# Gated-delta and gMLP decoder layer on one core: sample states loaded by the queue that stores them, right-hand sides of a head pair made together, one query tile earlier in the fill list

## The chip, the core and the metric

The kernel runs on one core of one Trainium2 chip. The metric is the device time of one execution in microseconds; smaller is better. The engines are TensorE (PE, with its weight loads as PEld), VectorE (DVE), ScalarE (ACT), GpSimd (POOL) and SyncE (SP). Each works through its own queue in order. DMA transfers are issued from the queues of SP, POOL and, twice, ACT.

## The reference, cut to what is touched

One layer of a decoder, for a prompt group (one sequence of 512 tokens) and a sample group (8 sequences of 8 new tokens each), which share all weights. The model has 1024 channels, 8 heads of 128 x 128 and float32 throughout.

```
h    = rms_norm(x);  proj = h @ w_in          # q,k,v | z | a,b | u,v | gates
q,k,v = silu(short causal conv of width 4), q and k of unit norm
# gated delta rule, per head, in chunks:
#   S_t = exp(g_t) (I - beta_t k_t k_t^T) S_{t-1} + beta_t k_t v_t^T,   o_t = S_t^T q_t
a_mat = strict_lower(k_beta @ k^T * decay)
sol   = triangular_solve(a_mat + I, [v * beta, k_beta * exp(gc)])
...                                            # scan over chunks; state of every sequence is an output
o_a  = rms_norm(o) * silu(z)
o_b  = u * (tril(W_s) @ layer_norm(v) + b)     # chunked gMLP branch
merged = sigmoid(g_a) * (o_a @ w_proj_a) + sigmoid(g_b) * (o_b @ w_proj_b)
x    = x + rms_norm(merged @ w_out);  x = x + rms_norm(swiglu_ffn(rms_norm(x)))
```

For the sample group the delta rule starts from a stored state, `state_delta`, one 128 x 128 matrix for each of 8 sequences and 8 heads, and returns the updated ones.

## The kernel before

All 576 tokens (64 sample, 512 prompt) stand side by side in the free dimension. Products run in three passes of a high and a low part (`xh`, `xl` against `whi`, `wlo`). A weight tile is 1024 x 128: SP loads it (`wunit_raw`, L261, 512 KB, two buffers `wraw`), ACT makes `whi`, DVE makes `wlo` (`wsplit`, L256 and L124), PE runs 24 matmuls for each of two halves of the tokens (`part`, L282), and the half is evicted from PSUM. PSUM has eight banks: three for weight tiles (`mmps`), five for everything else (`bank`). `ev` (L120) is a ring of seven SBUF tiles for short use: evictions, convolutions, gates, decay rows.

The stretch around the change is the delta branch. `delta(h0)` makes a set of steps for four heads, once for heads 0 to 3 (`dA`), once for 4 to 7 (`dB`). `keys` builds norms and Gram matrices (`decay`, L674, loads a row of decays `gcr` from the DRAM tile `gcd` by POOL, into `ev`). `elim` inverts 32 x 32 blocks on DVE. `combine` stores the result to DRAM, loads it back (`XH` by POOL, `XT` and `XS` by SP) and joins the blocks with small matmuls (L817 first). `scan` runs over the chunks of the prompt. `sample(q)` handles two heads `pr` of the sample group, so there are four calls in all; `both` takes turns between `scan` and `sample`. `output` scales and transposes the result (L975, L984), and `keys2` prepares the second four heads. These are Python generators: `main` steps through them one after the other.

Weight tiles that don't depend on this chain (keys and queries `kq`, values `va` and `vb`, gates `ga` and `gb`, `z`) are put between its steps: `FILL` names for each tile the number of the step of `main` behind which it is traced. Steps 13 to 23 belong to `elim` of `dA`, 24 to 28 to `combine` of `dA`. The order of tracing is a priority. A planner then fixes the order of every queue: on each engine it takes, of what is ready by its own clock and has a free buffer, what was traced first. So a queue's order isn't that of the text, and instructions can run far ahead of their place in it.

`sample(q)` loads four states `Si` (two heads, two halves `z` of four sequences, 256 KB each; four buffers) by `ld`, which is SP's queue. They are read by L880, updated in place and stored to `sd_s` by `st`, which is POOL's queue (L911). A state load of the next call needs a buffer whose store has landed. The update of one head and half is: copies that form W3 (`stack_w`, L720), the right-hand side `we` on DVE (96 x 512, one buffer), one matmul on PE (L907), four updates of 128 x 128 on DVE, the store. The helpers `tt` and `stt` record on L124 and L127, `act` on L136, whoever calls them.

Of the kernel before, what the change touches and what calls it, by code (L numbers as in the profile page):

```python
# [7 lines left out]
F32R = mybir.dt.float32r  # L8
# [4 lines left out]
P = 128  # L13
# [19 lines left out]
def _host_consts():  # L33
# [37 lines left out]
FILL = {  # L71
# [21 lines left out]
def _build(ctx, tc, I, O):  # L93
    nc = tc.nc
    V, S, G, TE = nc.vector, nc.scalar, nc.gpsimd, nc.tensor
    ld = nc.sync.dma_start
    st = nc.gpsimd.dma_start
# [19 lines left out]
    def bank():  # L117
        return pg.tile([P, 512], F32, name="bank", tag="bank")

    def ev(w=T):  # L120
        return evp.tile([P, 611], F32, name="ev", tag="ev")[:, :w]

    def tt(out, a, b, op):
        return V.tensor_tensor(out=out, in0=a, in1=b, op=op)  # L124

    def stt(out, a, s, b, op0, op1):
        V.scalar_tensor_tensor(out=out, in0=a, scalar=s, in1=b, op0=op0, op1=op1)  # L127
# [7 lines left out]
    def act(out, a, f, scale=1.0, accum=None):  # L135
        return S.activation(out=out, in_=a, func=f, scale=scale, accum_out=accum)  # L136
# [25 lines left out]
    def c(n):  # L162
        o, (r, w) = CONST_OFF[n]
        return con[:r, o - co0:o - co0 + w] if n in LATE else con2[:r, o - co1:o - co1 + w]
# [14 lines left out]
    for q in range(2):  # L179
        ps = bank()  # L180
# [54 lines left out]
    for t in range(5):  # L235
# [5 lines left out]
        if t in (1, 2, 3):  # L241
            ps = bank()
# [6 lines left out]
    ps = bank()  # L249
# [96 lines left out]
    pw = ExitStack()  # L346
# [81 lines left out]
    with tc.issue_after(last["v"].ins):  # L428
        ld(out=wsn, in_=I["w_spatial"][0].rearrange("g i j -> i g j"))
        ld(out=bsp.rearrange("p g i -> p (g i)"),  # L430
           in_=I["b_spatial"].rearrange("l g i -> l (g i)")[0].partition_broadcast(P))
# [13 lines left out]
    for q in range(2):  # L445
        ps = bank()
# [4 lines left out]
    ps = bank()  # L451
# [126 lines left out]
    def dt_(shape, nm, bufs=1, dt=F32):  # L578
        return dp.tile(shape, dt, name=nm, tag=nm, bufs=bufs)

    sct = dt_([P, 24, 27], "sct")
    for q in range(3):
        scn = dt_([24, D], "ae", 1)
        st(out=scn, in_=I["state_conv"][0].rearrange("s r f -> (s r) f")[:, q * D:(q + 1) * D])
        ps = bank()
# [20 lines left out]
    def jk():  # L606
        return dt_([P, P], "jk", 1, BF16)
# [42 lines left out]
    def delta(h0):  # L650
# [4 lines left out]
        L = Delta()  # L655
# [60 lines left out]
        def stack_w(w2, z):  # L716
            W3 = dt_([96, 2, P], "W3", dt=F32R)
            rows = slice(32 * z, 32 * z + 32)
            for r in (0, 64) if z == 0 else (0, 32, 64):
                S.copy(out=W3[r:r + 32], in_=w2[rows])  # L720
            tt(W3[32:64], w2[rows], W3[rows], ALU.subtract)
            return W3

# [142 lines left out]
        def sample(q):  # L866
            pr = (2 * q, 2 * q + 1)
            Vps, oS, CC = L.Vps, L.oS, L.CC
            Si = {}
            px = bank()  # L870
            for i, hh in enumerate(pr):
                for z in range(2):
                    Si[i, z] = dt_([P, 4, P], "Si", 4)
                    ld(out=Si[i, z], in_=I["state_delta"][0, 4 * z:4 * z + 4, h0 + hh].rearrange("s k v -> k s v"))
                for o_, f in ((0, F[1, hh]), (8, F[0, hh])):
                    V.tensor_copy(zv[:, o_:o_ + 8, 0:8], f[:, :NS].rearrange("p (s e) -> p s e", e=8))
                for s in range(4):
                    for j in range(4):
                        js = slice(32 * j, 32 * j + 32)
                        TE.matmul(px[js, i * P:(i + 1) * P], lhsT=ZT[:, j * 160 + 32 * s:j * 160 + 32 * s + 32], rhs=Si[i, j % 2][:, s],  # L880
                                  start=(s == 0), stop=(s == 3))
            yield
            rq = dt_([P, 2, P], "rq", 1)
            for i, hh in enumerate(pr):
                stt(rq[:NS, i], px[:NS, i * P:(i + 1) * P], EGN[:NS, 0, h0 + hh:h0 + hh + 1], Vps[:, hh],
                    ALU.mult, ALU.add)
            S.copy(out=rq[NS:P], in_=px[NS:P, 0:256].rearrange("p (a b) -> p a b", b=P))
            for i, hh in enumerate(pr):
                TE.matmul(px[:NS, 256 + i * P:256 + (i + 1) * P], lhsT=XS[:, hh], rhs=rq[:NS, i], start=True, stop=True)
            w2 = rq[:NS]  # L890
            tt(w2, px[:NS, 256:512].rearrange("p (a b) -> p a b", b=P),
               CC[:NS, 0, pr[0]:pr[0] + 2].unsqueeze(2).broadcast_to([NS, 2, P]), ALU.mult)
            for i, hh in enumerate(pr):
                TE.matmul(px[NS:P, i * P:(i + 1) * P], lhsT=L.ans[:, hh], rhs=w2[:, i], start=True, stop=True)
            yield
            tt(oS[:, pr[0]:pr[0] + 2], px[NS:P, 0:256].rearrange("p (a b) -> p a b", b=P), rq[NS:P], ALU.add)
            for hh in pr:
                act(jk()[NS:P], oS[:, hh], AF.Square, accum=SSO[NS:P, 0, h0 + hh:h0 + hh + 1])
            for z in range(2):
                W3 = stack_w(w2, z)  # L900
                for i, hh in enumerate(pr):
                    h = h0 + hh
                    we = dt_([96, 4, P], "we", dt=F32R)
                    tt(we, W3[:, i].unsqueeze(1).broadcast_to([96, 4, P]),
                       c("seqm4").unsqueeze(2).broadcast_to([96, 4, P]), ALU.mult)
                    ps = bank()
                    TE.matmul(ps, lhsT=L.KS[:, z, hh], rhs=we.rearrange("p s v -> p (s v)"), start=True, stop=True)  # L907
                    for s in range(4):
                        sq = 4 * z + s
                        stt(Si[i, z][:, s], Si[i, z][:, s], EGS[:, sq, h:h + 1], ps[:, s * P:(s + 1) * P], ALU.mult, ALU.add)  # L910
                    st(out=O["sd_s"][0, 4 * z:4 * z + 4, h].rearrange("s k v -> k s v"), in_=Si[i, z])  # L911
                yield
# [490 lines left out]
    def tile_mm(t):  # L1403
        T_[t] = Tile_(t, [mmt(), bank()])
        return T_[t].ps
# [11 lines left out]
    ps = tile_mm(0)  # L1417
# [4 lines left out]
    ps = tile_mm(2)  # L1422
# [9 lines left out]
    ps = tile_mm(3)  # L1432
# [7 lines left out]
    ps = tile_mm(4)  # L1440
# [39 lines left out]
    p, q = prs[2].banks("p"), prs[2].banks("q")  # L1480
# [166 lines left out]
```

## Time and profile before

| | |
|---|---|
| median of three runs | 1226.68 us (1223.93 to 1229.81) |
| profiled execution | 1224.94 us, of which the span is 1222.8 us |
| PE busy, share of the span | 1150.5 us, 94% |
| DVE busy | 717.4 us, 59% |
| ACT busy | 569.9 us, 47% |
| POOL busy | 149.7 us, 12% |
| mean granted clock of PE | 0.969 |

The profile is of one execution. The profiled time is the span from the first to the last instruction and 2.1 us around it. In time lines and wait lists a time in brackets is how long the engine stood idle before the instruction, and the name behind `<-` is what ended that. PE's granted clock is given as a share of 2.4 GHz; a stretch at 0.50 runs at 1.2 GHz. The weight-tile stages before 205 us make the normed input, the gMLP branch and its projection; from 205 to 690 us the delta branch runs between weight tiles; then follow `w_proj_a`, `w_out` and from 760 us the feed-forward network.

### The profile page before, as it was taken

How to read it: one execution, taken by the hardware profiler on the slowest of the kernel's cores; microseconds unless marked ns; L12 is line 12 of the kernel's file. 1: busy time of each engine (PE TensorE's matmuls, PEld its weight loads, DVE VectorE, ACT ScalarE, POOL GpSimd, SP SyncE). 2: the span in 40 equal slices, each digit the busy share in tenths (PEclk: the TensorE clock that was granted, in tenths of full speed). 3: DMA queues.
4: the chain of work that ended last, by engine and by line, in shares of the span. 5: the costliest groups of instructions: out<-in, count | busy, mean ns of one | idle time of the engine just before them, and what ended most of it. 6: DMA issues, size and time to landing. Idle time of an engine off the chain costs nothing.

```text
span 1222.8 us, 20426 instructions
## 1 busy us (share of the span) xinstructions
PE 1150.5 (94%) x8144; PEld 1075.6 (88%) x8144; DVE 717.4 (59%) x1386; ACT 569.9 (47%) x1227; POOL 149.7 (12%) x230
## 2 busy tenths in 40 slices
PE   6999999999997999999998998969999999899997
PEld 5999999998996998988997886858999999888885
DVE  4329722557873456767554664667777787661323
ACT  5423323884544773558445443435445445441221
POOL 3001210002000021020010100150111111160001
PEclk9999999999997998998999999988999999999999
DMA  6911344443344354654252744023233333212222
GB/s 163 220 59 37 85 127 112 76 88 110 91 110 94 80 132 91 171 131 89 67 137 72 260 136 138 2 68 87 87 93 92 93 104 103 87 53 86 86 87 78
DMA packets 163011, 124.74 MB, mean 102 GB/s; under 512 B 14096, under 2 KB 145713, under 8 KB 162916
## 3 DMA queue, kind: packets, MB, share of 16 engines
q1 hardware_dynamic: 156226, 103.72, 32.8%
q0 software_dynamic: 6544, 19.64, 4.9%
q8 instruction: 64, 1.05, 0.3%
q14 instruction: 31, 0.25, 0.1%
q10 hardware_dynamic: 146, 0.07, 0.0%
HBM read 106.35 MB, written 17.06 MB: 101 GB/s over the span
## 4 chain that ended last, share of the span: by engine, by line
PE 52%; DMA 7%; DVE 5%; ACT 4%; issue 2%; POOL 0%; POOLq 0%; DVEq 0%; ACTq 0%; SPq 0%
PE mmps L282 13%; PE bank L1305 10%; PE mmps L1305 7%; PE bank L1580 6%; PE mmps L1580 6%; DMA wraw<-w_in 2%; PE bank L1198 2%; PE mmps L1198 1%; DVE wlo L124 1%; DMA wraw<-w_out 1%; ACT whi L256 1%; DMA wraw<-w_proj_a 1%; DMA wraw<-w_ffn_out 1%; PE bank L880 1%; DMA XH<-d 1%
## 5 line engine op out<-in xcount | busy, mean ns | idle before, releaser
L282 PE MATMUL mmps<-xh,whi 128*128 128x256 f32 (+1 forms) x896 | 273.3, 305 | 4.8 <-ACT ev L136 2.9
L282 PE MATMUL mmps<-xh,wlo 128*128 128x256 f32 (+1 forms) x896 | 271.8, 304 | 4.5 <-DVE wlo L124 4.5
L282 PE MATMUL mmps<-xl,whi 128*128 128x256 f32 (+1 forms) x896 | 271.8, 304 | 0.0
L124 DVE TENSOR_TENSOR wlo<-wraw,whi 128x1024 fp32r<-128x1024 f32 x114 | 146.6, 1287 | 208.9 <-ACT whi L256 208.7
L256 ACT CAST whi<-wraw 128x1024 fp32r<-128x1024 f32 x114 | 119.3, 1047 | 209.4 <-PE mmps L282 60.2
L282 PEld LDWEIGHTS mmps<-xh,whi 128*128 128x128 f32 x896 | 174.3, 195 | 7.5 <-ACT ev L136 4.1
L282 PEld LDWEIGHTS mmps<-xh,wlo 128*128 128x128 f32 x896 | 174.4, 195 | 6.3 <-DVE wlo L124 5.6
L282 PEld LDWEIGHTS mmps<-xl,whi 128*128 128x128 f32 x896 | 174.3, 195 | 0.7 <-issue 0.3
L127 DVE SCALAR_TENSOR_TENSOR ev<-ev,fcol 128x600 f32<-128x600 f32 x72 | 60.1, 837 | 1.8 <-ACT ev L136 0.6
L136 ACT ACT_TABLE_LOAD x40 | 51.3, 1283 | 7.6 <-DVE ans L124 3.2
L1305 PE MATMUL bank<-mh,w2hi 128*128 128x288 f32 x156 | 48.0, 308 | 5.3 <-ACT w2hi L256 5.2
L1305 PE MATMUL bank<-mh,w2lo 128*128 128x288 f32 x156 | 47.5, 305 | 2.3 <-DVE w2lo L124 2.3
L136 ACT ACTIVATE ev<-mmps 128x320 f32<-128x320 f32 (+1 forms) x73 | 30.8, 431 | 38.0 <-PE mmps L282 26.4
L1305 PE MATMUL bank<-ml,w2hi 128*128 128x288 f32 x156 | 47.3, 303 | 0.0
L1283 POOL TENSOR_TENSOR wup<-wraw,wup 128x512 f32<-128x512 f32 x20 | 26.2, 1308 | 172.5 <-DVE wup L1283 150.6
L136 ACT ACTIVATE jk<-bank 128x128 bf16<-128x128 f32 (+1 forms) x112 | 31.2, 279 | 17.6 <-PE bank L952 11.6
L282 PE MATMUL mmps<-obl,whi 128*128 128x320 f32 (+1 forms) x128 | 38.6, 303 | 0.0
L282 PE MATMUL mmps<-obh,wlo 128*128 128x320 f32 (+1 forms) x128 | 38.4, 303 | 0.0
L282 PE MATMUL mmps<-oal,whi 128*128 128x320 f32 (+1 forms) x128 | 37.5, 295 | 0.8 <-DVE oal L124 0.8
L282 PE MATMUL mmps<-oah,wlo 128*128 128x320 f32 (+1 forms) x128 | 37.6, 297 | 0.7 <-DVE wlo L124 0.7
L282 PE MATMUL mmps<-oah,whi 128*128 128x320 f32 (+1 forms) x128 | 37.1, 298 | 0.7 <-ACT oah L310 0.7
L282 PE MATMUL mmps<-obh,whi 128*128 128x320 f32 (+1 forms) x128 | 37.6, 303 | 0.0
(501 smaller groups left out, 2996.3 us busy)
## 6 DMA issues: line engine op xcount, KB each, us to landing
wraw<-w_in SPq DMA_DIRECT2D x56, 512.0 KB, 8.2
wup<-w_ffn_in SPq DMA_DIRECT2D x22, 512.0 KB, 4.6
wraw<-w_ffn_out SPq DMA_DIRECT2D x22, 512.0 KB, 3.7
wraw<-w_ffn_in SPq DMA_DIRECT2D x20, 512.0 KB, 4.0
pgd<-ev POOLq DMA_DIRECT2D x16, 288.0 KB, 5.3
ev<-pgd SPq DMA_DIRECT2D x16, 288.0 KB, 7.8
wraw<-w_proj_b SPq DMA_DIRECT2D x8, 512.0 KB, 4.5
Si<-state_delta SPq DMA_DIRECT2D x16, 256.0 KB, 4.9
```

The source lines that it names most:

```text
L124: return V.tensor_tensor(out=out, in0=a, in1=b, op=op)
L127: V.scalar_tensor_tensor(out=out, in0=a, scalar=s, in1=b, op0=op0, op1=op1)
L136: return S.activation(out=out, in_=a, func=f, scale=scale, accum_out=accum)
L256: a = S.copy(out=hi, in_=raw)
L282: TE.matmul(ps, lhsT=a[:, j, :], rhs=b[k][:, HF[hf]], start=(k == 0 and i == 0), stop=(k == nk - 1 and i == 2))
L880: TE.matmul(px[js, i * P:(i + 1) * P], lhsT=ZT[:, j * 160 + 32 * s:j * 160 + 32 * s + 32], rhs=Si[i, j % 2][:, s], start=(s == 0), stop=(s ...
L1198: TE.matmul(ps[q], lhsT=a[k] if t == 0 else a[k][:, o:o + P], rhs=b[k][:, q * 512:(q + 1) * 512], start=(k == 0 and i == 0), stop=(k == KT ...
L1283: (G if g else V).tensor_tensor(out=out, in0=a, in1=b, op=op)
L1305: TE.matmul(ps, lhsT=w[x][:, j], rhs=b[y][:, j], start=(first and j == 0 and i == 0), stop=(j == KH - 1 and i == 2), skip_group_check=not ...
L1580: TE.matmul(ps, lhsT=x[k] if t == 0 else x[k][:, o:o + P], rhs=unit[w][:, a_], start=(k == 0 and i == 0), stop=(k == FT - 1 and i == len(t ...
```

## The change

Three edits. The state loads of `sample` are issued by `st` (POOL's queue) in place of `ld` (SP's). For each half `z` both heads' right-hand sides are made first, the second in an `ev` tile, with a bank of PSUM each; both matmuls follow their right-hand sides, and only then come the updates and stores of both heads. And the sixth entry of `kq` in `FILL`, the query tile of the second head of `dB`, goes from step 28 to step 24.

```diff
     "va": [8, 13, 23, 34],
-    "kq": [16, 20, 20, 24, 24, 28, 32, 33],
+    "kq": [16, 20, 20, 24, 24, 24, 32, 33],
     "ga": [53, 55, 69, 78, 78, 94, 105, 109],
...
                     Si[i, z] = dt_([P, 4, P], "Si", 4)
-                    ld(out=Si[i, z], in_=I["state_delta"][0, 4 * z:4 * z + 4, h0 + hh].rearrange("s k v -> k s v"))
+                    st(out=Si[i, z], in_=I["state_delta"][0, 4 * z:4 * z + 4, h0 + hh].rearrange("s k v -> k s v"))
...
             for z in range(2):
                 W3 = stack_w(w2, z)
+                we = [dt_([96, 4, P], "we", dt=F32R), ev(512).bitcast(F32R)[:96].rearrange("p (s v) -> p s v", v=P)]
+                pw = {}
                 for i, hh in enumerate(pr):
-                    h = h0 + hh
-                    we = dt_([96, 4, P], "we", dt=F32R)
-                    tt(we, W3[:, i].unsqueeze(1).broadcast_to([96, 4, P]),
+                    tt(we[i], W3[:, i].unsqueeze(1).broadcast_to([96, 4, P]),
                        c("seqm4").unsqueeze(2).broadcast_to([96, 4, P]), ALU.mult)
-                    ps = bank()
-                    TE.matmul(ps, lhsT=L.KS[:, z, hh], rhs=we.rearrange("p s v -> p (s v)"), start=True, stop=True)
+                    pw[i] = bank()
+                    TE.matmul(pw[i], lhsT=L.KS[:, z, hh], rhs=we[i].rearrange("p s v -> p (s v)"), start=True, stop=True)
+                for i, hh in enumerate(pr):
+                    h, ps = h0 + hh, pw[i]
                     for s in range(4):
```

## Rows read from the trace of the kernel before

**Rows 1.** A stretch: us; busy us and count by engine, PEclk, DMA share, GB/s.
```profile
205.00:690.00 485.00, 455.32 (x3782) 434.15 (x3781) 301.43 (x744) 281.36 (x744) 47.43 (x76) 0.96 0.43 104
```

**Rows 2.** Waits of PE, 205 to 690 us: total, times, longest.
```profile
PE bank L817 <- DMA XH<-d: 7.2, 1, 7.2
PE bank L907 <- DVE we L124: 5.7, 3, 3.5
...
PE bank L937 <- DVE R L127: 2.8, 1, 2.8
```

**Rows 3.** Time line of PE: start us, us, instruction, idle before it.
```profile
546.62 0.31 PE L282 MATMUL mmps<-xh,wlo 128*128 128x320 f32 x1
548.16 0.51 PE L907 MATMUL bank<-we,KS 96*128 96x512 f32 x1 [1.24 <-DVE we L124]
552.14 0.79 PE L907 MATMUL bank<-we,KS 96*128 96x512 f32 x1 [3.47 <-DVE we L124]
552.86 0.69 PE L975 MATMUL bank<-ident,vo 64*128 64x64 f32 x4
```

**Rows 4.** Time line of DVE in the same stretch.
```profile
547.43 0.68 DVE L124 TENSOR_TENSOR we<-W,con 96x512 fp32r<-96x512 f32 x1
...
550.37 1.11 DVE L127 SCALAR_TENSOR_TENSOR Si<-Si,egs,bank 128x128 f32<-128x128 f32 x4
551.40 0.68 DVE L124 TENSOR_TENSOR we<-W,con 96x512 fp32r<-96x512 f32 x1
```

**Rows 5.** Stretches at a low clock (busy of PE, PEld, DVE, ACT, POOL; PEclk).
```profile
380.00:396.00 16.00, 16.00 (x201) 15.76 (x200) 4.12 (x6) 7.65 (x10) 0.57 (x1) 0.64 0.22 55
552.00:560.00 8.00, 7.86 (x39) 6.83 (x40) 3.54 (x12) 5.75 (x15) 1.51 (x2) 0.57 0.42 76
668.00:672.00 4.00, 3.52 (x15) 3.52 (x16) 3.73 (x13) 2.04 (x4) 0.75 (x1) 0.57 0.82 223
```

**Rows 6.** Time line of PE in the last `sample` and behind it.
```profile
667.34 0.50 PE L907 MATMUL bank<-we,KS 96*128 96x512 f32 x1 [0.99 <-DVE we L124]
...
681.99 0.67 PE L282 MATMUL mmps<-oah,whi 128*128 128x320 f32 x3 [0.68 <-ACT oah L310]
683.44 0.41 PE L282 MATMUL mmps<-oal,whi 128*128 128x320 f32 x1 [0.78 <-DVE oal L124]
```

**Rows 7.** Waits of SP's DMA queue, 205 to 690 us.
```profile
SPq L874 <- DMA out_sd_s<-Si: 64.8, 11, 13.9
```

**Rows 8.** Time line of SP's DMA issues from 490 us.
```profile
494.33 3.03 SPq L874 DMA_DIRECT2D Si<-state_delta  x2
497.45 23.43 SPq L261 DMA_DIRECT2D wraw<-w_in  x4
```

**Rows 9.** Time line of DVE: the split that frees a `wraw` buffer.
```profile
492.33 1.23 DVE L124 TENSOR_TENSOR wlo<-wraw,whi 128x1024 fp32r<-128x1024 f32 x1 [1.89 <-ACT whi L256]
```

**Rows 10.** Instructions on the tile `Si`: ns min/median/max of the issue, first and last start.
```profile
L874 SPq DMA_DIRECT2D Si<-state_delta x16: 367/368/533, 148.8 to 637.4; - x16
L911 POOL DMA_DIRECT2D out_sd_s<-Si x16: 750/750/772, 462.2 to 679.1; - x16
```

**Rows 11.** Time line of POOL from 490 us: two of the decay loads.
```profile
493.42 0.56 POOL L677 DMA_DIRECT2D ev<-gcd  x1
...
565.84 0.55 POOL L677 DMA_DIRECT2D ev<-gcd  x1 [10.69 <-DVE an L124]
```

**Rows 12.** Time line of PE: the states of the second `sample` are first read.
```profile
520.60 1.08 PE L880 MATMUL bank<-Si,ZT 128*32 128x128 f32 x32
```

**Rows 13.** Time line of ACT: evictions of gate tile 3 and the query tile.
```profile
354.40 0.44 ACT L136 ACTIVATE ev<-mmps 128x320 f32<-128x320 f32 x1
...
358.57 0.20 ACT L618 COPY ev<-mmps 128x64 f32<-128x64 f32 x1
```

**Rows 14.** Time line of DVE: the gate's product, and one convolution step.
```profile
355.59 0.49 DVE L124 TENSOR_TENSOR ev<-ev 128x320 f32<-128x320 f32 x1 [0.84 <-DMA ev<-pgd]
...
357.02 0.83 DVE L127 SCALAR_TENSOR_TENSOR ev<-ev,fcol 128x600 f32<-128x600 f32 x1
```

## The prediction

> **What bounds the kernel now.** I read the stretches first, then TensorE's waits, then the time lines of the queues around each wait. TensorE (PE) is the bound: the stretch from 205 to 690 us, in which the delta branch runs between weight tiles, has 455.3 us of PE work in 485 us at a granted clock of 0.96 [rows 1]. So in the only stretch that the change touches, some 30 us are idle and 4% of the clock is not granted; the rest is work that the change neither adds nor removes. A gain must come out of waits that PE itself has. There are three to speak of: 7.2 us for the inverse's first blocks (L817), 5.7 us in three waits of L907 for the right-hand sides `we`, and 2.8 us for R of the scan [rows 2]. After the long idle times the granted clock falls to the lower of its two levels, 1.2 GHz, and for a while each PE instruction takes twice as long: the stretches 380 to 396, 552 to 560 and 668 to 672 us have a mean of 0.64, 0.57 and 0.57 [rows 5], which is 16 x 0.36 = 5.8, 8 x 0.43 = 3.4 and 4 x 0.43 = 1.7 us lost.
>
> **Part 2, both right-hand sides first.** Before, `we` has one buffer, and VectorE (DVE) gets RHS, four state updates, RHS, four updates. The second RHS of a half stands behind the updates of the first head, and these behind its matmul. PE meets this in the second `sample` of the first four heads: its last tile matmul ends at 546.93, then it waits 1.24 us, runs one L907, waits 3.47 us, runs the next, and only then turns to the transposes of L975 [rows 3]. On DVE, RHS at 547.43, updates at 550.37, RHS at 551.40 [rows 4]: what PE waits for are 0.68 us instructions, queued behind other work. After the change nothing but the copies of W3 stands between the two RHS, so both matmuls can run between tile matmuls before 546.93. That takes away 1.24 + 3.47 = 4.71 us, and the 0.28 us by which the matmul at 552.14 (0.79) was slower than the one before it (0.51) [rows 3]: 5.0 us. The half clock behind it (3.4 us) I don't count: ScalarE is busy 5.75 of these 8 us [rows 5] with copies that begin when L975 ends, and is next late. Bounds: nothing, since DVE works on without idle through the wait [rows 4] and none of its work goes away; 5.0 + 3.4 = 8.4 us at best.
>
> In the last `sample` the wait is 0.99 us, and the output behind the fourth L907 starts `w_proj_a` with waits of 0.68 and 0.78 us [rows 6]. Here no later fill covers. I take 0.99, half of 1.46 and half of the 1.7 us of clock: 2.5 us; bounds 0 and 0.99 + 1.46 + 1.7 = 4.2. In the two other calls PE has no wait at L907 (all three are named above), so their shorter chain is worth nothing.
>
> What it adds: a second bank of PSUM out of five, held some 1.1 us longer, and an `ev` tile for each of the eight pairs. `ev` is a ring of seven, for which the decay rows, the gates and the convolutions ask too. An RHS that finds none free stops DVE, and behind it the weight splits that PE waits for. Before, no RHS needs one. The nearest row is a decay load that waited 10.69 us until `an` gave one back [rows 11]. Bounds 0 and 10.69 each; I take 0, as an RHS holds its tile only until its matmul.
>
> **Part 1, the state loads on the storing queue.** SP waits 64.8 us in eleven waits until a stored state has landed, so that its buffer may be loaded again [rows 7], with weight loads behind it. Does PE pay for that? The clearest place: the loads at 494.33 end at 497.36, then comes a weight load at 497.45 [rows 8]. Its buffer was free when the split at 492.33 ended, at 493.56 [rows 9]: 3.9 us lost. But PE's one wait there is the one for R (2.8 us), not for weights. I take 0. The gain can be no more than 2.8.
>
> The same waits now stand in GpSimd's (POOL) queue, with the stores of gates, the decay loads and the stores of states behind them. Issue costs 750 ns there against 368 on SP [rows 10]: 16 x 0.38 = 6 us on an engine that is 47.4 us busy of 485 [rows 1], off the path. The load that hurts is the decay load at 493.42 [rows 11]: if both state loads go ahead of it, it leaves at 497.36 + 2 x 0.38 = 498.1, 4.7 us late, and DVE, in order, holds R for it. As it is issued before the first state load (493.42 against 494.33) I take 0; bounds -2.8 and +4.7. The loads themselves aren't urgent: those of 494 to 497 are first read at 520.60 [rows 12].
>
> All 16 stores of states from POOL took 750 to 772 ns to issue [rows 10], whatever DVE did beside them. The Trainium skill speaks against this part: "SBUF — State Buffer", section "SBUF: two separate sides", says that while DVE runs a copy of float32 within SBUF in its two-port mode, GpSimd can't write descriptors, and advises the SP or ACT queue. The 22 ns between the ends show no such hold here; by the page some of the 16 loads would go out later by as long as such a copy lasts, which the 23 us before their first reader would hide, and the sum would stay.
>
> **Part 3, the query tile at step 24.** The weight tiles run on PE in the order of the list, and PE takes them whenever the delta chain isn't ready. The fill moves ahead of combine's blocks and of gate tile 3 (step 26). But gate tile 3 and this query tile were evicted at 354.40 and 358.57 [rows 13], both long before 380, where the low-clock stretch behind the wait of L817 begins [rows 5]: the tile ran ahead of the blocks already. What changes is that the two swap, and with them on SP the tile's weight load and the gate's two loads (its weights and `pgd`), a place of one 512 KB load each way. The query tile's three convolutions (3 x 0.83 = 2.49 us) now fall into the elimination on DVE, which L817 awaits by way of two DMAs, in place of the gate's 0.49, some 0.39 (an estimate, 256 of 320 columns) and its wait of 0.84 [rows 14]: 0.8 us later. I take +0.8; bounds +2.5, and -13 (7.2 and 5.8 us of clock) if the planner does put more PE work ahead of L817.
>
> **Sum.** -5.0 - 2.5 + 0 + 0.8 = -6.7 us: the profiled execution goes from 1224.94 us (its span is 1222.8) to 1218.2. The median of the runs shown, 1226.68, lies 1.74 above it: 1218.2 + 1.74 = 1219.94, so 1220.
>
> **Rivals.**
> 1. *The stall only moves.* DVE has the same 64 updates and 16 RHS, and at 546 to 552 it is the busy engine; the scaled Vp come later, L984 waits instead of L907, or the decay load is held in POOL's queue (+4.7, sum -2.0). For it: no idle on DVE there. Against: PE waits on 0.68 us instructions alone. Time 1226.7 - 2.0 = 1224.7, up to 1228.
> 2. *Slower: the second RHS waits for an `ev` tile.* Place: the second `sample` of the first heads, when decay rows loaded ahead hold the ring. Price 10.69 us on DVE in place of the 4.71: -2.5 + 0.8 + (10.69 - 4.71) = +4.3, so 1231; twice, +15, so 1241.7; middle 1236. It decides from the point where such waits add up to more than 6.7 us uncovered. For it: the 10.69 us row. Against: a ring entry is asked for only while an RHS is under way.
> 3. *More than forecast: the new order also fills the wait of L817.* Half of its 13 us, so 1220 - 6.5 = 1213.5. For it: the order of all queues is made anew. Against: the tile in question already ran before.
> 4. *The change does nothing of what it says*, since the planner orders by readiness and places the instructions as before: 1226.7, within rival 1.
>
> **How the numbers follow.** Forecast 0.45 (own range 1215 to 1224), rival 1 with 4 0.21, rival 2 0.20, rival 3 0.14. 0.5% is 6.1 us, about what a measurement of this kernel can tell from no change, so "faster" is below 1220.5: 0.27 of the forecast's 0.45 and rival 3, 0.41. "Slower" is above 1232.8: most of rival 2, with its other end and a little of rival 1 making 0.22 in all. The same: 0.37. For 8 in 10 the range runs from 1209 (past rival 3's middle) to 1237 (past rival 2's): it leaves out the far halves of both.
>
> **What would show it.** Part 2 is right if L907 has no wait over 1 us and L975 of the first heads starts within 1 us of the last tile matmul; wrong if L984 or L975 waits instead for Vp or `vo`. Rival 2 shows as a wait of DVE, before an RHS, for a store or an `an`. Part 1: SP has no wait on a state's store, POOL has them, and the decay load near 493 leaves no later than two us after its `ev` is free; wrong if DVE waits over 3 us for it. Part 3: gate tile 3 is evicted after the query tile, and L817's wait stays between 7 and 9 us. The prediction is wrong if waits elsewhere in 205 to 690 us, which a new order of the queues can open, add up to more than the gain.

## The result and the profile after

The changed kernel takes 1236.11 us (median of six runs, 1233.30 to 1240.91) against 1227.26 for the kernel before beside it: ratio 1.0076, 95% interval 1.0051 to 1.0102. It is some 9 us slower, where 6.7 us faster was forecast. The profiled execution takes 1236.48 us, its span is 1234.7.

The same stretch as in [rows 1] and its low-clock stretches as in [rows 5] (busy us and count of PE, PEld, DVE, ACT, POOL; PEclk, DMA share, GB/s):

```profile
205.00:690.00 485.00, 443.00 (x3663) 421.16 (x3661) 295.27 (x735) 279.12 (x737) 55.85 (x87) 0.95 0.42 102
...
484.00:488.00 4.00, 3.82 (x18) 3.82 (x19) 3.79 (x10) 0.63 (x2) 1.19 (x2) 0.50 0.81 226
...
548.00:556.00 8.00, 6.75 (x35) 6.75 (x36) 7.39 (x19) 7.70 (x17) 0.52 (x1) 0.64 0.08 19
664.00:672.00 8.00, 6.96 (x33) 6.71 (x34) 5.83 (x19) 4.39 (x12) 1.32 (x2) 0.63 0.20 70
```

PE is busy 12.3 us less in the stretch than before, so 42 us are idle in place of 30. The low clock behind its long waits goes on costing as well: 4 x 0.50 = 2.0, 8 x 0.36 = 2.9 and 8 x 0.37 = 3.0 us in the three lower rows. Its waits there, where [rows 2] stood (total us, times, longest):

```profile
PE bank L939 <- DVE R L127: 8.6, 3, 6.4
PE bank L760 <- DVE vo L131: 6.6, 1, 6.6
PE bank L817 <- DMA XH<-d: 5.5, 1, 5.5
PE bank L907 <- DVE we L124: 4.6, 2, 2.7
PE mmps L282 <- ACT ev L136: 4.3, 5, 1.3
```

L939 is the L937 of before, two lines lower. The waits for the right-hand sides are not gone (4.6 us of 5.7, in other places), the wait for R has grown from 2.8 to 8.6, and 6.6 us for `vo` of the second heads' values are new. The time line of PE shows them, and that the inverse's first blocks now come in two pieces:

```profile
379.59 1.88 PE L817 MATMUL bank<-XH,at 32*32 32x32 f32 x32 [5.47 <-DMA XH<-d]
387.59 1.19 PE L817 MATMUL bank<-XH,at 32*32 32x32 f32 x32
484.18 1.22 PE L939 MATMUL bank<-R,XT 128*128 128x128 f32 x4 [6.42 <-DVE R L127]
510.76 0.50 PE L907 MATMUL bank<-we,KS 96*128 96x512 f32 x1 [1.89 <-DVE we L124]
549.25 2.08 PE L760 MATMUL bank<-f,f 128*128 128x128 f32 x8 [6.60 <-DVE vo L131]
665.04 0.80 PE L907 MATMUL bank<-we,KS 96*128 96x512 f32 x1 [2.72 <-DVE we L124]
```

DVE, at the same places, waits for DMAs that stand ahead of what PE wants:

```profile
362.41 0.49 DVE L124 TENSOR_TENSOR ev<-ev 128x320 f32<-128x320 f32 x1 [5.32 <-DMA ev<-pgd]
...
477.91 0.19 DVE L124 TENSOR_TENSOR tm<-ae,xe 72x31 f32<-72x31 f32 x1 [10.23 <-DMA ae<-d]
...
483.52 0.60 DVE L127 SCALAR_TENSOR_TENSOR R<-bank,gat,Vp 128x128 f32<-128x128 f32 x2
...
547.52 1.33 DVE L127 SCALAR_TENSOR_TENSOR ev<-ev,gat,con 64x64 f32<-64x64 f32 x5 [9.45 <-DMA ev<-gcd]
```

The first of them is the gate's product of [rows 14], which stood 0.84 us before. For the state loads, [rows 7] is gone from SP, and POOL waits instead, 31.5 us in eight waits of up to 10.3.

To see where the time goes, one profiled execution of each kernel is cut at two events: the end of the last L817 of the first heads, and the end of the last matmul of `w_proj_a` on `oah`. What follows the second is 490.4 to 493.9 us long in all sixteen. How much of such a time is scatter shows in kernels that have one order in all five queues up to L817. It starts between 377.6 and 379.5 in the kernel before, e2, e6 and e8, between 372.3 and 375.4 in e1, e5, e10, e13 and e14, at 381.4 and 384.2 in e7 and e9, and at 380.2 and 376.6 in e11 and e12: a single profile is good to some 3.6 us at that point. In the last column, e2 and e8 have one order in every queue to the end and differ by 3.4 us; e5 and e14, which differ by the order of the XH loads alone, by 4.8. A difference under 5 us in that column says nothing by itself.

| kernel | L817 starts | last L817 ends | `w_proj_a` ends | between them |
|---|---|---|---|---|
| before | 379.54 | 382.94 | 730.78 | 347.84 |
| after | 379.59 | 388.78 | 742.60 | 353.82 |
| e1 loads | 373.97 | 377.37 | 735.88 | 358.51 |
| e2 right-hand sides | 377.70 | 381.10 | 732.36 | 351.26 |
| e3 fill | 385.06 | 394.03 | 742.64 | 348.61 |
| e4 right-hand sides, fill | 384.39 | 393.13 | 746.32 | 353.19 |
| e5 first loads | 375.36 | 378.76 | 727.65 | 348.89 |
| e6 later loads | 377.56 | 380.96 | 741.16 | 360.20 |
| e7 fill, gate 3 | 381.35 | 390.60 | 739.15 | 348.55 |
| e8 ring tile | 379.43 | 382.83 | 737.52 | 354.69 |
| e9 fill, gate 3, XH | 384.20 | 387.68 | 738.28 | 350.60 |
| e10 loads, right-hand sides | 372.92 | 376.32 | 732.98 | 356.66 |
| e11 all, gate 3, XH | 380.21 | 383.61 | 732.30 | 348.69 |
| e12 first loads, fill, gate 3, XH | 376.63 | 380.03 | 731.75 | 351.72 |
| e13 first loads, right-hand sides | 375.06 | 378.46 | 728.46 | 350.00 |
| e14 first loads, XH | 372.30 | 375.70 | 729.41 | 353.71 |

The changed kernel is 11.8 us later at the second event: 5.8 of them are there when L817 ends; the 6.0 behind it are little more than that scatter.

### The profile page after: what moved, and what is told of

Same layout as the page of the kernel before. It is cut to its first block, busy times and chain, and to the rows that moved or that the text cites. A ratio compares the mean times of both kernels' runs of the same rounds, so it can differ in the third digit from the quotient of the medians.

```text
span 1234.7 us, 20437 instructions
## 1 busy us (share of the span) xinstructions
PE 1152.5 (93%) x8144; PEld 1077.2 (87%) x8144; DVE 716.9 (58%) x1386; ACT 573.7 (46%) x1229; POOL 162.7 (13%) x246
## 4 chain that ended last, share of the span: by engine, by line
PE 52%; DMA 5%; DVE 5%; ACT 4%; issue 3%; POOL 0%; POOLq 0%; DVEq 0%; ACTq 0%; SPq 0%
PE mmps L282 15%; PE bank L1307 9%; PE mmps L1307 7%; PE bank L1582 6%; PE mmps L1582 6%; PE bank L1200 2%; PE mmps L1200 1%; DMA ae<-d 1%; DMA ev<-gcd 1%; DMA wraw<-w_out 1%; ACT jk L136 1%; DVE wlo L124 1%; ACT whi L256 1%; DMA wraw<-w_ffn_out 1%; DMA wraw<-w_ffn_in 1%
## 5 line engine op out<-in xcount | busy, mean ns | idle before, releaser
L136 ACT ACTIVATE ev<-ev 128x576 f32<-128x576 f32 (+3 forms) x41 | 20.9, 539 | 35.2 <-DVE ev L127 28.6
```

## Experiments: one part at a time

Theory A: the loss comes from the right-hand sides, whose new order puts other work ahead of the scan. Theory B: from POOL's queue. Theory D: from the fill list. All edits are against the kernel before unless said.

**e1**, the state loads alone.

```diff
-                    ld(out=Si[i, z], in_=I["state_delta"]...
+                    st(out=Si[i, z], in_=I["state_delta"]...
```

> Only the state loads move from SP's queue to POOL's; right-hand sides and fill list are those of before. Theory A (the loss of some 9 us comes from the right-hand sides, which make the order of all queues behind the first sample anew): same as before, within 2 us, with PE's waits at L907 (5.7 us) and L817 (7.2 us) still there. Theory B (POOL's queue: decay loads and the loads of the inverse stand behind state loads that wait for a store): 5 to 9 us slower, with waits of DVE for decay loads (ev<-gcd) that grow by 5 us or more.

1231.27 us against 1223.18: 1.0060 (1.0037 to 1.0083). PE's wait for R is 12.5 us in place of 2.8, DVE's waits for decay loads are 15.3 in place of 3.5; L907's 5.7 are as before. So theory B has a case here, which the last column shows (358.51), though L817 comes 5.6 us earlier.

**e2**, the right-hand sides alone (the third block of the diff).

> Only the right-hand sides of both heads made first, the second in a tile of the ring; state loads on SP and the fill list of before. Theory A: slower by 5 to 12 us, with new waits of PE for R of the scan or for the second elimination, 5 us or more each, and the time of the waits at L907 not gained. Theory B: faster by up to 5 us, as predicted for this part. Theory C (an RHS waits for a tile of the ring): slower, and DVE waits 5 us or more ahead of an RHS (L124 we or ev from W).

1228.66 us: 1.0037 (1.0016 to 1.0059), slower by about 4.5. No wait of DVE for a ring tile ahead of an RHS. Neither A's new waits of 5 us nor B's gain: PE's waits are

```profile
PE bank L817 <- DMA XH<-d: 6.2, 1, 6.2
PE bank L939 <- DVE R L127: 5.9, 4, 3.0
PE mmps L282 <- DVE wlo L124: 4.6, 4, 2.9
PE bank L907 <- DVE we L124: 4.6, 2, 2.7
PE bank L946 <- ACT w L136: 3.3, 7, 0.5
```

R has 3.1 us more than before and `w` of the scan (L946, the L944 of before) 2.7 more, for 1.1 less at L907; PE is busy 451.08 us in the stretch in place of 455.32. The first heads' last L907 runs at 517.54 in place of 552.14, so the chain did get shorter; PE's idle time did not.

**e3**, the fill list alone.

> Only the query tile moved from step 28 to step 24 of the fill list. Prediction's own price: +0.8 us (bounds -13 and +2.5). Theory A: within 2 us of before. Theory D (the fill list is what costs: the gate tile falls behind L817's wait and the first sample starts later): 4 to 9 us slower.

1234.95 us: 1.0092 (1.0060 to 1.0124). The smallest edit is the dearest, 11.3 us: theory D, above its 4 to 9. In the table all of it is there when L817 ends (394.03 against 382.94), and the rest of the time line is as long as before. Here are SP's queue (start, length of the group, issues), DVE and PE:

```profile
325.52 27.59 SPq L261 DMA_DIRECT2D wraw<-w_in  x5
353.15 0.57 SPq L1011 DMA_DIRECT2D ev<-pgd  x1
...
366.61 0.49 DVE L124 TENSOR_TENSOR ev<-ev 128x320 f32<-128x320 f32 x1 [6.15 <-DMA ev<-pgd]
...
370.99 1.09 DVE L795 COPY ae<-xe 72x1024 f32<-72x1024 f32 x1
...
385.06 1.88 PE L817 MATMUL bank<-XH,at 32*32 32x32 f32 x32 [6.77 <-DMA XH<-d]
392.84 1.19 PE L817 MATMUL bank<-XH,at 32*32 32x32 f32 x32
```

The same in the kernel before (SP, DVE, PE):

```profile
326.15 20.84 SPq L261 DMA_DIRECT2D wraw<-w_in  x4
347.09 0.53 SPq L1011 DMA_DIRECT2D ev<-pgd  x1
...
363.23 1.11 DVE L795 COPY ae<-xe 72x1024 f32<-72x1024 f32 x1
...
379.54 3.40 PE L817 MATMUL bank<-XH,at 32*32 32x32 f32 x64 [7.17 <-DMA XH<-d]
```

Gate tile 3's `pgd` block is loaded behind five weight loads (before: behind four, at 347.09) and is there at 366.6. Its product stands in the middle of the elimination on DVE, which so ends 7.8 us later (the copy of L795 starts at 370.99; before at 363.23). And 26 tile matmuls run between the two halves of L817, many of them at 1.2 GHz, after the wait: the mean granted clock is 0.56 from 388 to 392 us.

**e4**, right-hand sides and fill list, so the change without its loads.

> Right-hand sides and fill list as in the changed kernel, state loads back on SP's queue. Theory A: as slow as the changed kernel, within 3 us of 1236 (+9 us). Theory B: 5 us or more faster than the changed kernel, so within 4 us of before.

1242.12 us: 1.0151 (1.0118 to 1.0184), slower than the changed kernel. Theory A's number would be 1236 and B's 1231 at most, so neither holds; the loads on POOL are thus no loss in the full change but a gain of 6 us or more (1242.12 against 1236.11; 9 by the ratios, each to its own runs of the kernel before). The waits for R (8.3) and for `vo` (7.8) stand here already, without any state load on POOL.

## Experiments: inside the parts

**e5**, only the four loads of the first `sample` by POOL, and **e6**, only the other twelve.

```diff
-                    ld(out=Si[i, z], in_=I["state_delta"]...
+                    (st if h0 + q == 0 else ld)(out=Si[i, z], ...   # e5
+                    (ld if h0 + q == 0 else st)(out=Si[i, z], ...   # e6
```

> Only the four state loads of the first sample call (148.85 us before) go to POOL's queue; the other twelve stay on SP, the rest is before. Theory Q (two effects of part 1 with opposite signs: the early loads off SP's queue gain some 5.6 us by L817, the later ones in POOL's queue hold back the decay load): L817 starts near 374 us, PE's wait for R stays at 2 to 4 us, total 4 to 6 us faster than before. Rival (the gain by 374 us is chance of that run, or is given back later): within 2 us of before.

> The other twelve state loads go to POOL's queue, the first four stay on SP's. The orders on PE, DVE and ACT are those of before to the instruction. Theory Q: L817 near 379.5 us as before, PE's wait for R grows from 2.8 to 10 us or more, DVE waits 10 us or more for that decay row, total 9 to 13 us slower than before. Rival (the growth comes from the changed order of PE, not from POOL's queue): wait for R under 5 us and the total within 3 us of before.

e5: 1221.95 us against 1226.18, ratio 0.9969 (0.9951 to 0.9987), faster by 3.8 us, a little under theory Q's 4 to 6. e6: 1234.12, ratio 1.0069 (1.0043 to 1.0095), slower by 8.5, under its 9 to 13, with PE, DVE and ACT in the order of before to the instruction. So part 1 holds two effects of opposite sign. The early one lies ahead of the stretch that the prediction read; the kernel before has there

```profile
154.20 0.65 PE L587 MATMUL bank<-ident,ae 24*128 24x24 f32 x8 [2.04 <-DMA Si<-state_delta]
...
150.00:162.00 12.00, 9.96 (x69) 9.54 (x69) 4.73 (x9) 3.50 (x7) 4.46 (x6) 0.86 0.54 144
```

and e5, in the same 12 us,

```profile
150.00:162.00 12.00, 11.97 (x91) 11.32 (x90) 6.93 (x14) 4.79 (x9) 8.13 (x11) 1.00 0.41 116
```

PE idles 2.0 us and runs at 0.86 before, and neither after. The releaser named is a state load; the transposes read `ae`, a load of the convolution state that POOL issues at 149.33, amid the four state loads, and that lands with them at 153.95. All sixteen traces show this: with these state loads on SP (eight kernels) that load of `ae` lands 3.6 to 4.6 us after its issue and PE waits 1.1 to 2.0 us ahead of the transposes; with them on POOL (the other eight), where they leave behind it, it lands after 2.4 to 2.8 us and PE waits 0.2 at most. In e5 those transposes also stand later in PE's order, so how much of the wait each of the two takes away is not shown.

The later effect, in e6 (POOL, DVE, PE):

```profile
500.72 0.75 POOL L874 DMA_DIRECT2D Si<-state_delta  x1 [8.83 <-DMA out_sd_s<-Si]
501.46 0.56 POOL L677 DMA_DIRECT2D ev<-gcd  x1
...
505.12 1.32 DVE L127 SCALAR_TENSOR_TENSOR ev<-ev,gat,con 64x64 f32<-64x64 f32 x5 [11.62 <-DMA ev<-gcd]
...
507.45 0.80 PE L937 MATMUL bank<-R,XT 128*128 128x128 f32 x2 [11.15 <-DVE R L127]
```

The decay load of [rows 11] leaves at 501.46 in place of 493.42: a state load ahead of it waits 8.83 us for a store to land. DVE waits for the decay row, R behind it, PE for R. "DMA: Bandwidth & Descriptors" of the Trainium skill, section "Anatomy of one DMA — SWDGE (gpsimd) path", says that the DMA engines do not wait on semaphores, the issuing sequencer does, before it dispatches. The two POOL rows agree: the wait of one load (8.83 us) is the lateness of the next (8.04).

**e7**, the fill list, with gate tile 3's `pgd` load on POOL; PE's and ACT's orders are e3's.

```diff
-        ld(out=pbt, in_=pgd[m])
+        (st if m == 3 else ld)(out=pbt, in_=pgd[m])
```

> Fill list of the change (query tile at step 24), everything else of before, but gate tile 3 loads its pgd block by POOL's queue, where no weight load stands ahead of it; the orders of PE and ACT are those of the fill list alone. Theory G (the loss of the fill list starts with that load, for which DVE waits 6.15 us in the middle of the elimination): that wait under 1 us, L817 at 380 us or earlier against 385.06, and 5 us or more of the 11.8 us given back. Theory F (there is less to fill behind L817, whatever the elimination does): L817 earlier, but PE waits more for it, and the total stays within 3 us of the fill list alone.

1233.68 us: 1.0059 (1.0039 to 1.0079). L817 starts 3.7 us earlier than in e3, 1.4 short of theory G's "380 or earlier", and its second half is still apart; e9, which has the same orders up to there, starts it only 0.9 us earlier than e3. The total gives back about 4 of 11, not 5, and its interval meets e3's. So theory G isn't shown, and DVE shows why it gains so little:

```profile
359.20 0.48 DVE L124 TENSOR_TENSOR ev<-ev 128x320 f32<-128x320 f32 x1
...
365.54 1.23 DVE L124 TENSOR_TENSOR wlo<-wraw,whi 128x1024 fp32r<-128x1024 f32 x1 [4.35 <-ACT whi L256]
...
367.83 1.14 DVE L795 COPY ae<-xe 72x1024 f32<-72x1024 f32 x1
```

The product waits no more, but a weight split whose tile has not landed now stands ahead of the last steps of the elimination: it ends 3.2 us earlier than in e3 (in e9 0.5) and 4.6 later than before. From 300 us to the copy of L795, DVE idles 9.2 us before, 14.6 in e3 and e4, and 12.6 and 12.4 in e7 and e9. Weight splits take 9.4 of it in the last two, 3.6 in e3. So most of the wait moves from the gate's load to weight tiles, and the `pgd` load alone is not its cause.

**e8**, the second right-hand side in a ring tile, all else in the text's old order.

```diff
-                    we = dt_([96, 4, P], "we", dt=F32R)
+                    we = (dt_([96, 4, P], "we", dt=F32R) if i == 0 else
+                          ev(512).bitcast(F32R)[:96].rearrange("p (s v) -> p s v", v=P))
```

> The update loop of before, in its order, but the second head's right-hand side in a tile of the ring ev rather than in the one buffer we. So it need not wait for the first matmul, and nothing is written out first. Theory A (any edit here makes the order behind it anew, with a result of either sign): not within 1 us of before, and its waits at L907 and for R differ from those of both before and the right-hand sides alone. Theory B (the second buffer by itself takes the waits at L907 away): L907 waits under 2 us and the total 2 to 5 us faster. Theory C (ring): DVE waits 5 us or more for a tile.

1229.52 us: 1.0025 (1.0008 to 1.0042). The waits at L907 are 4.6 us in two places, as in e2, those for R 4.1 in three. All five queues have e2's order, instruction by instruction. So a second buffer alone is part 2; "made first" in the text adds nothing, and what differs between e2 and e8 (1.0037 and 1.0025, 5.9 and 4.1 us for R) is scatter. Theory A, an order of its own, and theory B fall. There is no wait for a tile: theory C and with it the prediction's rival 2 fall. A buffer outside the ring was not tried.

**e9**, e7 with the blocks of XH loaded in the order 0, 2, 1, so that both halves of L817 get their data early.

```diff
-            for b in range(2):
+            for b in (0, 2, 1):
                 bs_ = slice(b * NB, (b + 1) * NB)
-                st(out=XH[bs_, :, bs_], in_=d2[0, b * NM:(b + 1) * NM]...
-            st(out=XH[64:96, :, 0:NB], in_=d2[0, 2 * NM:3 * NM]...
+                xd = XH[bs_, :, bs_] if b < 2 else XH[64:96, :, 0:NB]
+                st(out=xd, in_=d2[0, b * NM:(b + 1) * NM]...
```

> As the kernel with the fill list and gate tile 3's load on POOL, and combine loads the third block of XH (rows 64 to 96) ahead of the second, so that the two halves of L817 have their data one behind the other; L817 then stands in one piece in PE's order. Theory T (the rest of the fill list's loss is that the planner puts 26 tile matmuls between the halves of L817, 7 us of PE at a low clock): L817 ends near 385 us or earlier against 390.60, and the total is within 3 us of before. Rival (fewer tiles behind L817): L817 whole, but the total stays 5 us or more slower than before, with waits at L907 of 11 us or more.

1230.96 us against 1224.77: 1.0053 (1.0032 to 1.0073). L817 is in one piece, but theory T misses both its numbers: it starts at 384.20 and ends at 387.68, the total stays 6 us up, and the waits at L907 are 16.4 us (5.7 to 6.4 where neither fill list nor right-hand sides are touched). With the right-hand sides of before, the query tile taken early seems to leave PE without cover there, as the rival said.

**e10**, loads and right-hand sides, so the change without its fill list.

> Loads and right-hand sides as in the changed kernel, fill list of before. If the costs simply add (+7.4 for the loads alone, +4.5 for the right-hand sides alone): 12 us slower than before. If the order made by the right-hand sides puts no state load ahead of a decay load that is needed soon, only the early gain (about -4) and the right-hand sides' cost are left: within 3 us of before. Either way 6 us or more of the changed kernel's loss goes with the fill list only in the second case.

1224.86 us: 1.0012 (0.9989 to 1.0035). Without the move of one query tile the change is neutral. The costs don't add (7.3 + 4.5 would be 12).

**e11**, the changed kernel in full, with e7's and e9's edits.

> The changed kernel in full, with gate tile 3's load on POOL and the third block of XH ahead of the second. Theories G and T together: L817 in one piece, ending 6 us or more earlier than the changed kernel's 388.78, and the total 6 to 10 us below the changed kernel, so within 4 us of before. Rival (the loss sits behind L817, in the waits for R and vo): within 3 us of the changed kernel, those waits unchanged.

1224.40 us: 0.9994 (0.9976 to 1.0012), some 10 us below the changed kernel by the ratios.

```profile
380.21 3.40 PE L817 MATMUL bank<-XH,at 32*32 32x32 f32 x64 [7.28 <-DMA XH<-d]
...
PE bank L939 <- DVE R L127: 7.3, 3, 5.1
...
PE bank L760 <- DVE vo L131: 2.4, 1, 2.4
```

L817 starts no earlier than in the changed kernel (380.21 against 379.59) and, being in one piece, ends 5.2 us earlier; 5.1 more are saved behind it, about the scatter of that column, 4.2 of them in the wait for `vo`. The theory's total holds, its 6 us at L817 are 5.2; the rival, which had the later waits unchanged, falls. The two edits were not run one without the other in the changed kernel, but as L817 starts no earlier, the gain there comes from its one piece rather than from the `pgd` load, as far as one profile tells.

**e12**, first loads on POOL, fill list, e7's and e9's edits.

> A version put together from what helped: the first call's state loads on POOL, the query tile at step 24, gate tile 3's load on POOL, the third block of XH ahead of the second; right-hand sides and later state loads as before. Theory (the query tile ahead gains nothing by itself, it only no longer costs): as the first call's loads alone, 2 to 5 us faster than before. Rival 3 of the prediction (the tile fills a part of L817's wait): that wait at 4 us or less, 7 us or more faster than before.

1226.57 us: 1.0009 (0.9989 to 1.0030), slower than e5. The wait of L817 is 6.8 us, so the tile fills nothing of it, and the waits at L907 are 16.4 as in e9. The theory was too kind: even repaired, the move costs 2 to 5 us (against e14 and e5) where the right-hand sides are those of before.

**e13**, first loads on POOL with the new right-hand sides, and **e14**, first loads with e9's order of XH.

> Right-hand sides as in the changed kernel, only the first call's four state loads on POOL's queue, the other twelve on SP's, fill list of before. Compared with the loads and right-hand sides together (+1.5 us): theory Q2 (in the order that the right-hand sides make, the twelve later loads on POOL cost nothing): within 2 us of that kernel. Rival (they cost there as they did alone, +8.5 us, and something else hid it): 5 us or more faster than that kernel, so 3 us or more faster than before.

> The first call's four state loads on POOL's queue, and the third block of XH loaded ahead of the second; the orders of PE, DVE, ACT and SP are those of the first call's loads alone. Does the order of the XH loads have a price of its own? Theory (none: L817 is in one piece there already): as that kernel, 2 to 5 us faster than before, L817's wait 6 to 7.5 us. Rival (it shortens the wait): L817's wait under 5 us and 6 us or more faster than before.

e13: 1222.54 us against 1223.73, 0.9990 (0.9972 to 1.0008). e14: 1223.39, 0.9990 (0.9976 to 1.0004). By their ratios e13 lies 2.7 us below e10, outside theory Q2's 2 and far from the rival's 5; the intervals overlap. So the twelve later loads cost from nothing to some 6 us in that order, and 8.5 alone; more isn't settled. One cost shows: PE waits 2.0 us for the states themselves (L880) in e10, 0.6 in e13. e14 has e5's orders on PE, DVE, ACT and SP, and L817's wait is 6.2 us as there: the order of XH has no price of its own there. By its ratio it gains 1.2 us, short of its theory's 2 to 5, where e5 gained 3.8 with the same orders: the early loads are worth 1 to 4 us. e5 is the one kernel whose interval lies below 1.

## Why the prediction was wrong

**Part 3 is the step that failed most**: +0.8 us (bounds -13 and +2.5) against 11.3 alone and some 8 in the change (1.0076 against e10's 1.0012). Three things in it were wrong. The prediction saw that the gate's loads and the query tile's trade places on SP, "a place of one 512 KB load each way", and gave that no price: its own row, the 0.84 us wait for `pgd` [rows 14], was struck out as if the wait went away with the swap. The product stayed in the elimination, and one place in SP's queue made 6.15 us of 0.84 (e3). Where the forecast took 0.84 us off, DVE's idle time up to L795 grew by 5.4, and with the gate's load out of SP's queue still by 3.3 (e7, e9). The trace of before had that price in it: the weight load that SP issues at 353.28 takes 13.6 us to land there, as gate tile 3's takes 13.4 from 353.15 in e3. Second, by "the tile ran ahead of the blocks already" it took the order of L817 itself as fixed; the planner put 26 tile matmuls between its halves. In the changed kernel this seems to count for most (e11). Third, a tile taken early seems to be missing later (e9, e12). The mark it set, "L817's wait stays between 7 and 9 us", was near (5.5) and blind: the wait of PE can be the same while the chain behind it is 11 us later.

**Part 2**: -7.5 us against +4.5 alone. That the second matmul would no longer wait behind updates held: in six of the eight halves both L907 now run within 0.6 us of each other, and L977 (the L975 of before) starts at 519.48 behind the tile matmul of 519.15. But its sign, no wait over 1 us at L907, failed (1.89 and 2.72), and the gain went into other waits: rival 1 in kind, the stall only moves, though not at the places that it named. DVE's time line of the kernel before:

```profile
466.24 0.60 DVE L127 SCALAR_TENSOR_TENSOR R<-bank,gat,Vp 128x128 f32<-128x128 f32 x2
476.61 0.19 DVE L124 TENSOR_TENSOR tm<-ae,xe 72x31 f32<-72x31 f32 x1 [9.77 <-DMA ae<-d]
476.72 1.22 DVE L124 TENSOR_TENSOR wlo<-wraw,whi 128x1024 fp32r<-128x1024 f32 x1
```

DVE waits there for `ae` of the second elimination too, but R is made ahead of that, and of what comes behind it PE waits for the weight split alone (3.0 us). In the changed kernel the same wait (10.23) has St, Si and R behind it, and PE idles 6.42 us. With part 2 alone R stands behind that wait too, but PE waits only 3.0 us for it in e2 and 1.5 in e8. DVE in e2:

```profile
475.41 0.19 DVE L124 TENSOR_TENSOR tm<-ae,xe 72x31 f32<-72x31 f32 x1 [11.77 <-DMA ae<-d]
...
482.61 0.60 DVE L127 SCALAR_TENSOR_TENSOR R<-bank,gat,Vp 128x128 f32<-128x128 f32 x2
```

So the 6.42 need the fill list beside part 2 (e4 has 6.1). The forecast priced the wait that it took away, and not the DVE instructions that the shorter chain would put behind a DMA. Rival 1 argued from a DVE without idle; the idle came from a DMA instead. Rivals 3 and 4 fall too: L817's wait is 5.5 to 7.7 us in every kernel, and the orders did change.

**Part 1**: 0 (bounds -2.8 and +4.7) against +7.3 alone. The failed step is "as it is issued before the first state load (493.42 against 494.33) I take 0": times of one queue's issues don't carry over to a queue with both. The price, PE's wait for R 8.4 to 9.8 us longer, is twice the bound, because the load ahead waited for a store that landed later than those of [rows 8]. And "the only stretch that the change touches" left out four of sixteen loads at 148.85 [rows 10], which give back 1 to 4 us, in a wait ahead of 205 us that was not read. As expected, SP's waits on stores were worth next to nothing to PE: its waits for splits are 3.9 us in e6, 4.5 before.

On issue cost it was right: all 32 issues of states on POOL take 749 to 813 ns in the changed kernel. The rule of the Trainium skill that was weighed there, "SBUF — State Buffer", section "SBUF: two separate sides", shows no hold longer than 64 ns in these rows.

**The sum** failed as its last sentence feared: waits elsewhere in the stretch. The parts aren't additive (7.3, 4.5 and 11.3 alone, 9 together), since each remakes an order in which the next is priced. The range, 1209 to 1237, held the time by luck: 1236 is the middle of rival 2, and no wait for a ring tile came. The chance of slower, 0.22, looks low for an edit that remakes every queue.

What stays open: whether the later loads cost anything in the order of the new right-hand sides, how e5's gain divides between the queue and the transposes' place, which of e11's two edits brings its 10 us, and why loads land late around 355 us. The account of part 2 is read from the rows; no run takes the waits named there away.

## What to carry to other kernels

When a load moves one place in a queue, find the instruction that waits for it and ask what stands behind that one on its in-order engine: 0.84 us of waiting inside a dependent chain became 6.15 with one 512 KB load more ahead, and with that load taken elsewhere most of the wait came back at the next weight tile. Look in the trace of before how long loads take to land at the time to which one is moved. Read the whole trace for every instruction that an edit moves, the first call's too, before calling a stretch the only one. And where a planner remakes the queues, run each part alone and each left out: three parts that cost 7, 4.5 and 11 us together cost 9, and one list entry held nearly all of it. Two runs of one order tell how small a difference between two profiles can be read.

## What the runs showed of the hardware

In these runs the size of a load did not set how long it takes to land. The median of the 288 KB `pgd` loads is 7.8 us from issue to landing in the profile of the kernel before, 4.5 in the changed kernel's and 8.2 in e3's; gate tile 3's took 13.4 us in e3 (from 353.15), with a 512 KB weight load issued just ahead of it and another behind. From 355 to 360 us all DMAs together moved 50 GB/s there, and 51 before; no run shows what held them. The Trainium skill, "DMA: Bandwidth & Descriptors", section "Anatomy of one DMA — SWDGE (gpsimd) path", fits 2.0 us and 436 KB per us for one DMA, which would make such a block's time about 2.7 us (an estimate, and for the other issue path); the measured times are 1.7 to 5 times that, and they decide here.

The load of `ae` shows one neighbour's part: 3.6 to 4.6 us to land with four state loads issued around it from another queue, 2.4 to 2.8 us without them.
